# Values' projections as one 512-column product over both weight halves, and another order of work for the soft-max heads, in a two-layer hybrid encoder

## The chip, the cores and the metric

The kernel runs on one core of one Trainium2 chip. The metric is the device time of one execution in microseconds; less is better. The core has a matrix engine (TensorE, PE in the profile, with its weight loads shown apart as PEld), VectorE (DVE), ScalarE (ACT), GpSimd (POOL) and a queue that issues DMAs (SP). PE multiplies a moving operand by a stationary one of 128 x 128 and adds into PSUM; ACT and DVE read PSUM, POOL does not.

## The reference

Two layers work on x of 512 tokens by 1024. Each layer makes one wide projection of x, runs two groups of eight heads on it (head size 64), gates them, projects back and normalises:

```
proj = x @ w_in          # qA kA vA gA | qB kB vB gB | qI kI wI
A[t,s] = sigmoid(z[t,s]) * prod_{s<j<t} (1 - sigmoid(z[t,j])),  s < t      # group A, "sticks"
oA = A @ vA
score[t,s] = sum_h wI[t,h] relu(qI[t,h] . kI[s])                           # group B, soft-max heads
keep the 128 best admissible s of each t;  p = softmax(q.k/8 + bias[bucket(s-t)])
oB = p @ vB
x = LayerNorm(alpha * x + concat(oA*silu(gA), oB*silu(gB)) @ w_out)
```

All in float32.

## The kernel before

**Precision by halves.** A float32 operand is split into a high half (rounded to the type that PE multiplies at full rate, `fp32r`) and a low half (the rest). A product is three: high x high, low x high, high x low. So x lies in SBUF as `XH` and `XL`, and every weight chunk is split as it arrives: `raw` from DRAM, `whi` by ACT (L212), `wlo` by POOL (L215). Class `Stream` (L173) does this ahead of use, with two raw buffers and four buffers each for `whi` and `wlo`; its loads go out on SP in order.

**Units.** A projection unit is 256 columns of `w_in` for half of a group: (A or B, which four heads, q, k, v or g). q, k and gate units (`project_t`, L276) hold the weights still and move 512 tokens of x. Value units (`project_v`, L286) hold 128 tokens of x still and move 256 weight columns, so that values come out with tokens on partitions: four token blocks `tb`, each of eight chunks `kc` of the contraction, each chunk three matmuls (L303 to L305) into one PSUM tile `pjv`. The first unit of a layer, (A, 0, v), is joined with the indexer's keys (328 columns, weights in `joined`); the other three value units, (A, 1, v), (B, 0, v) and (B, 1, v), stand alone. The block's result is taken from PSUM ("eviction") by closures in the list `later`, which `flush()` calls at fixed places: for A, one ACT copy to `V_NOW` (L310), and after the last block a shift of the values by one row through three DMAs (`shift_values`) with differences two slots later; for B, `evac_v`: an ACT copy to the high half (L358), a DVE subtraction to the low half (L359). PSUM tiles for projections rotate through three buffers (`ppj`).

**Slots.** The order on PE, ACT, DVE and POOL is that of the program text; nothing is reordered. A layer runs 88 tasks, one a slot `s` (loop at L887): 24 for the indexer, then 64 for sixteen heads by four query blocks `qb`; heads 0 to 7 are sticks, 8 to 15 soft-max. A task's work is spread over slots: its scores z (`stage0`, PE) in its own slot; for a stick, sigmoid on ACT and one slot later a running product on DVE, transposes on PE three slots later (L526), their eviction to the buffers `AT` by ACT and DVE (L715, L718); for a soft-max task, bias and row minimum on DVE (L750), exponential on ACT (L755) in its own slot, transposes two slots later (L534, L537 evict them). After a head's fourth block comes `values()`, eight matmuls of AT by the values into `o` (L693), and `mix()`, which adds o's two halves and multiplies them into `M` (L595 on ACT, L597 on DVE, L598 on POOL). For sticks `values()` comes one slot after the last transposes and right behind the slot's own transposes; for soft-max heads one slot after the last transposes too, but at the slot's end, behind the fill.

**Fill.** Between these steps `fill(t)` issues projection matmuls, chunk by chunk, until their count of work (324 for a value chunk, 648 for others) reaches a target that is interpolated between pins (`HEAD_PINS`, `A_PINS`, `B_PINS`); so each unit has its slots: (A, 1, v) 35 to 38, (B, 0, v) 55 to 61, (B, 1, v) 70 to 77, and from slot 78 the first part of the output projection (`p1`). `fill` is called at 0.15, 0.55 and 1 of the slot; the call at 0.15 is left out where a stick is to be transposed.

**Top-k and biases.** From slot 24 to 51 `topk_rounds` puts the indexer's selection on DVE (L842, L843), about 1.5 rounds a slot; it ends in `mask[qb]`. A soft-max head's bias for a block is a strip of a table in DRAM (`f_dram`), read with one address step per row (tile `gbias`, L662) and used reversed. For heads 8 to 12 and two blocks of 15, POOL adds the mask (L741) or PE does; for heads 13, 14 and the other two blocks of 15, `STORED` names a place in `XN` (free then) where DVE adds table and mask ahead (L959) in slots 59 to 66, from tiles loaded at slots 57, 60 and 64 (`AHEAD`).

**Tail.** From slot 77 on, `mix_split` splits finished rows of M into XH and XL (L166, L167) for the output projection, the residual comes back into XN, and weights of `w_out` are split.

## Time and profile before

| what | value |
|---|---|
| median of 3 runs | 635.69 us (635.49 to 635.9) |
| the profiled execution | 635.7 us, span 633.9 us, granted clock 0.997 |
| PE busy | 624.9 us, 99% of the span |
| PEld, DVE, ACT, POOL busy | 547.0, 486.9, 343.2, 364.1 us |
| DMA | 77.41 MB, mean 122 GB/s |
| value matmuls of 256 columns (L303, L304, L305) | 192 each |

The span runs from the first to the last instruction of the profiled execution; the 1.8 us beside it are launch and end. A row of instructions names line, engine, operation, output and inputs with their shapes, how many there are, their busy time and the mean of one in ns, then the engine's idle time ahead of them and what ended it. In a timeline row the first figure is the start, the second the duration, and the bracket the idle time before it with its releaser. Matmuls overlap in the pipeline, so their spacing is read from starts. `z` are scores, `tr` transposes, `o` a head's output, `pj` and `pjv` projections, `pjo` the output projection.

### The profile page before, as it was taken

The numbers are of one execution on the slowest core, as the hardware profiler recorded it, in microseconds if no ns is written. First come the engines' busy times: TensorE is split into PE (matmuls) and PEld (weight loads), VectorE is DVE, ScalarE is ACT, GpSimd is POOL, SyncE is SP. The second block draws the span as 40 slices with busy tenths as digits, with TensorE's granted clock in tenths as the row PEclk, the third lists the DMA queues.
The fourth block names the chain that finished last, engine by engine and source line by source line (L and its number), as shares of the span: only waits on it lengthen the run. The fifth ranks groups of instructions, "written<-read, shape, count | busy, mean of one in ns | idle before, by whom it ended". The sixth has DMA issues, their size and how long they took to land.

```text
span 633.9 us, 10261 instructions
## 1 busy us (share of the span) xinstructions
PE 624.9 (99%) x3501; PEld 547.0 (86%) x3501; DVE 486.9 (77%) x1058; ACT 343.2 (54%) x686; POOL 364.1 (57%) x380
## 2 busy tenths in 40 slices
PE   9999999999999999999999999999999999999995
PEld 7988888988889889888899888899888898898884
DVE  3778999999966775668845789999998576656677
ACT  5686545544447466883135855554535566668700
POOL 5463544467466676798134544525674587778721
PEclk9999999999999999999999999999999999999998
DMA  7624343222263475353314342333133624634502
GB/s 237 214 79 133 100 133 101 82 86 68 99 169 94 120 188 168 119 192 119 133 67 132 103 132 99 100 100 106 62 101 116 167 85 137 173 126 144 168 34 99
DMA packets 31779, 77.41 MB, mean 122 GB/s; under 512 B 6572, under 2 KB 10668, under 8 KB 31728
## 3 DMA queue, kind: packets, MB, share of 16 engines
q1 hardware_dynamic: 31440, 76.51, 39.0%
q8 instruction: 27, 0.44, 0.3%
q10 hardware_dynamic: 288, 0.26, 0.1%
q14 instruction: 24, 0.20, 0.1%
HBM read 61.84 MB, written 4.44 MB: 105 GB/s over the span
## 4 chain that ended last, share of the span: by engine, by line
PE 92%; POOL 2%; ACT 2%; DMA 1%; DVE 1%; issue 1%; SPq 0%; DVEq 0%; POOLq 0%; ACTq 0%
PE pj L266 15%; PE pj L267 15%; PE pj L268 15%; PE pjo L797 12%; PE o L693 5%; PE tr L526 5%; PE z L521 4%; PE pjv L303 4%; PE z L518 4%; PE pjv L304 4%; PE pjv L305 4%; PE pjv L428 2%; POOL wlo L215 1%; PE pjq L430 1%; ACT p L755 1%
## 5 line engine op out<-in xcount | busy, mean ns | idle before, releaser
L215 POOL TENSOR_TENSOR wlo<-raw,whi 128x256 fp32r<-128x256 f32 (+1 forms) x250 | 225.0, 930 | 152.6 <-ACT whi L212 151.9
L266 PE MATMUL pj<-XH,whi 128*128 128x512 f32 (+1 forms) x432 | 171.5, 397 | 0.0
L267 PE MATMUL pj<-XL,whi 128*128 128x512 f32 (+1 forms) x432 | 166.4, 385 | 0.0
L268 PE MATMUL pj<-XH,wlo 128*128 128x512 f32 (+1 forms) x432 | 166.2, 385 | 0.0
L268 PEld LDWEIGHTS pj<-XH,wlo 128*128 128x128 f32 x432 | 81.1, 188 | 16.1
L267 PEld LDWEIGHTS pj<-XL,whi 128*128 128x128 f32 x432 | 81.4, 188 | 12.2
L266 PEld LDWEIGHTS pj<-XH,whi 128*128 128x128 f32 x432 | 81.3, 188 | 12.3
L705 ACT ACTIVATE om<-z 128x128 f32<-128x128 f32 (+1 forms) x64 | 28.0, 437 | 113.7 <-PE z L521 60.8
L212 ACT ACTIVATE whi<-raw 128x1024 fp32r<-128x1024 f32 x78 | 82.0, 1056 | 8.0 <-DMA raw<-in_w_in_dram 7.4
L598 POOL TENSOR_TENSOR M<-M,mixt 64x512 f32<-64x512 f32 x24 | 40.5, 1689 | 52.7 <-DVE mixt L597 41.3
L710 DVE TENSOR_TENSOR_SCAN om<-om,future 128x128 f32<-128x128 f32 (+1 forms) x64 | 63.6, 994 | 0.1
L303 PE MATMUL pjv<-whi,XH 128*128 128x256 f32 x192 | 56.9, 296 | 0.0
L305 PE MATMUL pjv<-wlo,XH 128*128 128x256 f32 x192 | 54.2, 283 | 0.0
L304 PE MATMUL pjv<-whi,XL 128*128 128x256 f32 x192 | 54.2, 282 | 0.0
L842 DVE MAX8 m<-scores 128x8 f32<-128x256 f32 (+2 forms) x96 | 52.8, 550 | 0.2
L843 DVE MATCH_REPLACE8 scores<-m,scores 128x256 f32<-128x256 f32 (+2 forms) x96 | 52.1, 543 | 0.0
L755 ACT ACTIVATE p<-p,mn 128x128 f32<-128x128 f32 (+1 forms) x64 | 35.8, 559 | 20.2 <-DVE mn L750 19.9
L693 PE MATMUL o<-AT,vt 128*128 128x512 f32 (+4 forms) x256 | 46.2, 322 | 0.0
L521 PE MATMUL z<-k,q 128*128 128x128 f32 (+3 forms) x128 | 41.7, 326 | 0.0
L797 PE MATMUL pjo<-whi,XH 128*128 128x512 f32 (+1 forms) x118 | 41.1, 387 | 0.0
L797 PE MATMUL pjo<-wlo,XH 128*128 128x512 f32 (+1 forms) x118 | 41.1, 384 | 0.0
L537 DVE TENSOR_TENSOR AT<-tr,AT 128x128 fp32r<-128x128 f32 (+1 forms) x64 | 31.2, 488 | 11.5 <-ACT AT L534 11.2
(165 smaller groups left out, 1286.7 us busy)
## 6 DMA issues: line engine op xcount, KB each, us to landing
raw<-in_w_in_dram SPq DMA_DIRECT2D x66, 512.0 KB, 3.3
k<-k SPq DMA_DIRECT2D x32, 256.0 KB, 5.5
raw<-in_w_out_dram SPq DMA_DIRECT2D x14, 512.0 KB, 3.2
gbias<-f_dram SPq DMA_DIRECT2D x18, 256.0 KB, 3.2
XN<-in_x_dram SPq DMA_DIRECT2D x8, 256.0 KB
y_dram<-XN SPq DMA_DIRECT2D x4, 512.0 KB, 2.6
XN<-y_dram SPq DMA_DIRECT2D x8, 256.0 KB, 3.7
M<-M SPq DMA_DIRECT2D x4, 448.0 KB
```

The lines of the kernel that those rows point to most:

```text
L212: A.activation(hi, src, AF.Copy)
L215: low = lambda lo=lo[:, c], src=src[:, c], hi=hi[:, c]: lo_engine.tensor_tensor(lo, src, hi, ALU.subtract)
L266: T.matmul(o, w[0], XH[:, tb:, kc, :], start=first, stop=False)
L267: T.matmul(o, w[0], XL[:, tb:, kc, :], start=False, stop=False)
L268: T.matmul(o, w[1], XH[:, tb:, kc, :], start=False, stop=last)
L303: T.matmul(full, XH[:, tb, kc, :], whi, start=kc == 0, stop=False)
L304: T.matmul(full, XL[:, tb, kc, :], whi, start=False, stop=False)
L305: T.matmul(full, XH[:, tb, kc, :], wlo, start=False, stop=kc == KC - 1)
L521: T.matmul(self.z[:, :nn], c, d, start=False, stop=True)
L693: T.matmul(self.o[:m, sb * P :], vt[:, sb, self.hh * P : self.hh * P + m], at_block(self.at[j], sb, sb, NTB - sb), start=n == 0, stop=n == 7)
L710: V.tensor_tensor_scan(rev, rev, future[:, S - n :][:, ::-1], 1.0, ALU.mult, ALU.max)
L797: T.matmul(acc[:, cols], mixed[:, tb, m, :], w[:, cols], start=n == 0, stop=n == len(steps) - 1)
```

## The change

1. **Value units that stand alone.** Their two weight halves are kept side by side: tile `w` of 2048 (formerly `whi` and `wlo` of 1024) is viewed as chunk, half, column, and `Stream.split` writes its two outputs there. A chunk's matmuls become two: XH by both halves, 512 columns, into the whole PSUM tile; XL by the high half, 256 columns, into its first half. In the last chunk the order is turned, so that the wide one ends the group. The two halves of the PSUM tile are added at eviction: `add_rest` copies the second half by ACT and adds it by DVE, for A straight into `V_NOW`, for B back into PSUM, with `evac_v` behind it. The joined first unit and all other units multiply as before.
2. **Slots.** For slots below 86, no fill at 0.15 where any task is to be transposed, and `values()` right behind the transposes for soft-max heads too; these come two slots after the last transposes now instead of one, and `mix()` with them. The last slots keep the old order.
3. **Stored biases.** The strips are loaded straight to their places in XN at slots 42, 44 and 46 (ten DMAs a layer), and DVE adds the masks in place, two sums a slot from slot 52. The three whole-width loads of `AHEAD` go away; the strips are read reversed where they are used.

```diff
--- before.py
+++ after.py
@@ -61,11 +61,12 @@
 
 
 STORED = {
-    13: {3: (59, 3, 0), 2: (59, 2, 0), 1: (60, 1, 0), 0: (60, 2, 384)},
-    14: {3: (62, 0, 512), 2: (62, 1, 512), 1: (63, 2, 512), 0: (63, 1, 896)},
-    15: {3: (66, 3, 512), 1: (66, 2, 768)},
+    13: {3: (3, 0), 2: (2, 0), 1: (1, 0), 0: (2, 384)},
+    14: {3: (0, 512), 2: (1, 512), 1: (2, 512), 0: (1, 896)},
+    15: {3: (3, 512), 1: (2, 768)},
 }
-AHEAD = {13: 57, 14: 60, 15: 64}
+STORE_SLOTS = {42: 13, 44: 14, 46: 15}
+SUM_AT = 52
 RESIDUAL = {(0, 0): 70, (0, 1): 78, (0, 2): 79, (0, 3): 80, (1, 1): 83, (1, 0): 84, (1, 2): 86, (1, 3): 88}
 SUM_SLOTS = 3
 HALF_SLOTS = 5
@@ -170,8 +171,15 @@
         nc.sync.dma_start(dst.bitcast(F32), src.bitcast(F32))
 
 
+    def weight_pair(name):
+        return wp.tile([P, 2048], F32R, tag="w", name=f"w{name}")
+
+    def halves(w):
+        return w[:, :1024], w[:, 1024:]
+
     class Stream:
-        def __init__(self, specs):
+        def __init__(self, specs, side_by_side):
+            self.side_by_side = side_by_side
             self.specs, self.raw, self.done, self.home = specs, {}, {}, {}
             self.loaded = self.ready = self.want = 0
             self.shared = set()
@@ -203,9 +211,13 @@
             if i in self.home:
                 pieces = self.home[i]
             else:
-                pieces = [[wp.tile([P, 1024], F32R, tag=tag, name=f"{tag}{i}") for tag in ("whi", "wlo")]]
-                self.done[i] = tuple(pieces[0])
-                pieces = [[t[:, :n].rearrange("p (a b) -> p a b", b=raw.shape[2]) for t in pieces[0]]]
+                w = weight_pair(i)
+                if i in self.side_by_side:
+                    self.done[i] = w = w.rearrange("p (a j b) -> p a j b", j=2, b=raw.shape[2])
+                    pieces = [[w[:, :, j, :] for j in range(2)]]
+                else:
+                    self.done[i] = halves(w)
+                    pieces = [[t[:, :n].rearrange("p (a b) -> p a b", b=raw.shape[2]) for t in self.done[i]]]
             k = raw.shape[1] // len(pieces)
             for j, (hi, lo) in enumerate(pieces):
                 src = raw[:, j * k : (j + 1) * k]
@@ -236,17 +248,19 @@
 
     units = [("A", 0, "v"), "ki", ("I", 0, "q")] + [u for u, _ in fills()]
 
-    specs, index = [], {}
+    specs, index, side_by_side = [], {}, set()
     for l in range(depth):
         for unit in units:
             index[l, unit] = len(specs)
             if unit == "ki":
                 specs.append((w_ki[l], 8 * 72))
             else:
+                if unit[2] == "v" and unit != units[0]:
+                    side_by_side |= {len(specs), len(specs) + 1}
                 specs += [(w_in[l, UNITS.index(unit), c], 1024) for c in range(2)]
         index[l, "o"] = len(specs)
         specs += [(w_out[l, half, mt], 1024) for half in range(2) for mt in range(4)]
-    stream = Stream(specs)
+    stream = Stream(specs, side_by_side)
 
 
     later = []
@@ -287,34 +301,46 @@
         i = index[l, unit]
         if keys is None:
             stream.prep(i + 1)
-            w = [[t.rearrange("p (a b) -> p a b", b=W256) for t in stream.done[i + h]] for h in range(2)]
+            w = [stream.done[i + h] for h in range(2)]
         else:
             stream.prep(i + 2)
             w = joined
-        n = w[0][0].shape[2]
         vv = vt.rearrange("p t (h r) -> p t h r", r=P)
         for tb in range(NTB):
             if tb:
                 stream.want = i + min(tb + 1, 3) + (keys is not None)
-            full = ppj.tile([P, S], F32, tag="pj", name="pjv")[:, :n]
-            acc = full[:, :W256]
+            full = ppj.tile([P, S], F32, tag="pj", name="pjv")
+            n = w[0][0].shape[2] if keys is not None else S
+            acc, rest = full[:, :W256], full[:, W256:]
             for kc in range(KC):
-                whi, wlo = (t[:, kc % 4, :] for t in w[kc // 4])
-                T.matmul(full, XH[:, tb, kc, :], whi, start=kc == 0, stop=False)
-                T.matmul(full, XL[:, tb, kc, :], whi, start=False, stop=False)
-                T.matmul(full, XH[:, tb, kc, :], wlo, start=False, stop=kc == KC - 1)
+                x = [t[:, tb, kc, :] for t in (XH, XL)]
+                if keys is not None:
+                    whi, wlo = (t[:, kc % 4, :] for t in w[kc // 4])
+                    products = ((full[:, :n], x[0], whi), (full[:, :n], x[1], whi), (full[:, :n], x[0], wlo))
+                else:
+                    both = w[kc // 4][:, kc % 4]
+                    products = ((full.rearrange("p (a b) -> p a b", b=W256), x[0], both), (acc, x[1], both[:, 0]))
+                    if kc == KC - 1:
+                        products = products[::-1]
+                for m, (o, a, b) in enumerate(products):
+                    T.matmul(o, a, b, start=kc == m == 0, stop=(kc, m) == (KC - 1, len(products) - 1))
                 if kc == KC - 1:
                     if keys is not None:
                         later.append(lambda tb=tb, full=full: keep_keys(tb, full))
-                    if unit[0] == "A":
                         later.append(lambda tb=tb, acc=acc: A.activation(V_NOW[:, tb, :], acc, AF.Copy))
+                    elif unit[0] == "A":
+                        later.append(lambda tb=tb, acc=acc, rest=rest: add_rest(V_NOW[:, tb, :], V_NOW[:, tb, :], acc, rest))
                     else:
+                        later.append(lambda tb=tb, acc=acc, rest=rest: add_rest(acc, tp.tile([P, S], F32, tag="t", name="rest")[:, :W256], acc, rest))
                         later.append(lambda tb=tb, acc=acc: evac_v(vv, tb, acc))
                 if (tb, kc) == (NTB - 1, KC - 1) and unit[0] == "A":
                     later.append(shift_values)
                     pending.append([SHIFT_SLOTS[1], lambda: value_steps(vv)])
-                yield 324 * n // W256
-
+                yield 324 * n // W256 if keys is not None else 324
+
+    def add_rest(out, place, acc, rest):
+        A.activation(place, rest, AF.Copy)
+        V.tensor_tensor(out, place, acc, ALU.add)
 
     V_NOW, V_PREV = (M[:, i : i + 2, :].rearrange("p x (y d) -> p (x y) d", d=W256) for i in (6, 4))
     pending = []
@@ -389,7 +415,7 @@
         unit = [index[0, u] for u in units[:3]]
         q_raw = vp.tile([P, NTB, 4 * P], F32, tag="v", name="q_raw").rearrange("p (c a) b -> p c (a b)", c=2)
         vk_raw = M.rearrange("p a b -> p (a b)")[:, : KC * (W256 + 72)].rearrange("p (a b) -> p a b", b=W256 + 72)
-        q_w = [tuple(wp.tile([P, 1024], F32R, tag=tag, name=f"{tag}q{c}") for tag in ("whi", "wlo")) for c in range(2)]
+        q_w = [halves(weight_pair(f"q{c}")) for c in range(2)]
         bias["oh"] = kp.tile([P, 4, S], F32, tag="k", name="oh").rearrange("p a b -> p (a b)")
         accs = [ppj.tile([P, S], F32, tag="pj", name="pjv") for _ in range(3)]
         q_accs = [pz.tile([P, S], F32, tag="z", name="pjq") for _ in range(2)]
@@ -656,10 +682,13 @@
                 return q, self.s, k, 2 * self.s
 
             def load(self):
+                self.g = gp.tile([P, S], F32, tag="g", name="gbias")
+                self.fetch(self.g)
+
+            def fetch(self, place):
                 h = 4 * self.i + self.hh
-                self.g = gp.tile([P, S], F32, tag="g", name="gbias")
                 base = f_dram[h : h + 1, 0:S]
-                nc.sync.dma_start(self.g, bass.AP(tensor=base.tensor, offset=base.offset, ap=[[1, P], [1, S]]))
+                nc.sync.dma_start(place, bass.AP(tensor=base.tensor, offset=base.offset, ap=[[1, P], [1, place.shape[1]]]))
 
             def begin(self):
                 self.late = (self.pair, self.s) != (7, 1)
@@ -733,8 +762,8 @@
                 self.p = wk.tile([P, S], F32, tag="w", name="p")
                 self.apart = bool(stored) and self.qb not in stored
                 if self.qb in stored:
-                    _, tb, col = stored[self.qb]
-                    self.bias = XN[:, tb, col : col + self.n]
+                    tb, col = stored[self.qb]
+                    self.bias = XN[:, tb, col : col + self.n][:, ::-1]
                     return
                 self.bias = h.g[:, : self.n][:, ::-1]
                 if not self.apart:
@@ -833,6 +862,7 @@
                 else:
                     st["done"] += step
 
+        sums = []
         rounds = [qb for _ in range(TOPK // 8) for qb in range(1, NTB)]
 
         def topk_rounds(upto):
@@ -896,9 +926,10 @@
                     stream.prep_ahead()
             now = s + (s >= IDX_SLOTS)
             sticks = [at(s - i) if isinstance(at(s - i), Stick) else None for i in (3, 4)]
-            softs = [at(s - i) if isinstance(at(s - i), Soft) else None for i in (2, 3)]
+            softs = [at(s - i) if isinstance(at(s - i), Soft) else None for i in (2, 4 if s < SLOTS - 2 else 3)]
             olds = [t for t in (sticks[0], softs[0]) if t]
             ended = [t if t and t.qb == NTB - 1 else None for t in (sticks[1], softs[1])]
+            joined_run = bool(olds) and s < SLOTS - 2
             done = ended[0] or ended[1]
             if at(s):
                 tasks[s].stage0()
@@ -911,12 +942,12 @@
             if isinstance(at(s + 1), Soft):
                 tasks[s + 1].prepare()
             flush()
-            if not sticks[0]:
+            if not joined_run:
                 fill(now + FRAC[0])
             for old in olds:
                 old.transpose()
                 old.evacuate(old.head.at)
-            if ended[0]:
+            if done and s < SLOTS - 2:
                 done.head.values()
             if behind:
                 tasks[s - 1].stage2()
@@ -935,7 +966,7 @@
                 stream.home[o0 + 10] = [[t[:, :, W256:] for t in joined[i]] for i in range(2)]
                 lows = []
                 stream.split(o0 + 8, lows=lows)
-            if ended[1]:
+            if done and s >= SLOTS - 2:
                 done.head.values()
             if done:
                 mix(done.head.pair, done.head.s, done.head.o, V if last else G)
@@ -950,13 +981,15 @@
             for place, by in RESIDUAL.items():
                 if s == by:
                     load_residual(l, *place)
-            for h in STORED:
-                if s == AHEAD[h]:
-                    by_number[h].load()
-                for qb, (by, tb, col) in STORED[h].items():
-                    if s == by:
-                        n = P * (qb + 1)
-                        V.tensor_tensor(XN[:, tb, col : col + n], by_number[h].g[:, :n][:, ::-1], mask[qb], ALU.add)
+            if s in STORE_SLOTS:
+                h = STORE_SLOTS[s]
+                for qb, (tb, col) in STORED[h].items():
+                    by_number[h].fetch(XN[:, tb, col : col + P * (qb + 1)])
+                    sums.append((XN[:, tb, col : col + P * (qb + 1)], mask[qb][:, ::-1]))
+            if s >= SUM_AT:
+                for place, hidden in sums[:2]:
+                    V.tensor_tensor(place, place, hidden, ALU.add)
+                del sums[:2]
             if l == 0 and s in (10, 14):
                 make_future(s == 14)
             if l == 0 and s in (3, 6):
```

## The prediction

> **What bounds the kernel now.** I read the page first (engine totals, granted clock, chain), then the waits of the weight loads, then single rows of the timeline.
>
> ```profile
> span 633.9 us, 10261 instructions
> PE 624.9 (99%) x3501; PEld 547.0 (86%) x3501; DVE 486.9 (77%) x1058; ACT 343.2 (54%) x686; POOL 364.1 (57%) x380
> ...
> PEclk9999999999999999999999999999999999999998
> ...
> PE 92%; POOL 2%; ACT 2%; DMA 1%; DVE 1%; issue 1%; SPq 0%; DVEq 0%; POOLq 0%; ACTq 0%
> ```
>
> TensorE is busy 99% of the span at full clock and is 92% of the chain. Its weight loads wait for other engines at a handful of places only:
>
> ```profile
> PEld tr L526 <- ACT p L765: 1.2, 3, 0.5
> ...
> PEld o L693 <- DVE AT L537: 0.3, 2, 0.2
> PEld tr L526 <- ACT p L755: 0.3, 2, 0.2
> ```
>
> So time is won by shortening TensorE's own stream, and lost wherever another engine falls behind it. Busy rows overstate a matmul (they are pipelined); what counts is start to start:
>
> ```profile
> 200.74 0.28 PE L303 MATMUL pjv<-whi,XH 128*128 128x256 f32 x1
> 200.85 0.28 PE L304 MATMUL pjv<-whi,XL 128*128 128x256 f32 x1
> 200.97 0.28 PE L305 MATMUL pjv<-wlo,XH 128*128 128x256 f32 x1
> ...
> 202.17 0.28 PE L303 MATMUL pjv<-whi,XH 128*128 128x256 f32 x1
> ```
>
> ```profile
> 151.69 0.39 PE L266 MATMUL pj<-XH,whi 128*128 128x512 f32 x1
> ...
> 153.74 0.39 PE L266 MATMUL pj<-XH,whi 128*128 128x512 f32 x1
> ```
>
> ```profile
> 71.23 0.39 PE L268 MATMUL pj<-XH,wlo 128*128 128x512 f32 x1
> 71.46 0.28 PE L518 MATMUL z<-k,q 128*128 128x256 f32 x1
> 71.57 0.28 PE L521 MATMUL z<-k,q 128*128 128x256 f32 x1
> 71.69 0.40 PE L266 MATMUL pj<-XH,whi 128*128 128x512 f32 x1
> ```
>
> From 200.74 to 202.17 lie 12 matmuls of 256 columns: 1.43 / 12 = 119 ns each, 357.5 ns a chunk of three. From 151.69 to 153.74 lie 9 of 512: 228 ns each. The third fence is the only place where 256 columns follow 512: 110 and 120 ns.
>
> **The change part by part.**
>
> *Matmuls.* 6 units (three value projections in each of two layers) x 4 token blocks x 8 chunks = 192 chunks; the rows of the eviction groups below count their blocks, 8 (of the 12 at L310) and 16. A chunk goes from 3 x 256 columns to 512 + 256: the same columns, one weight load and one matmul fewer. New form, so bounds: 228 plus 110 to 120 is 338 to 348; I take 228 + 117 = 345, since half the 256-column matmuls will have a 512 on both sides as at 71.57. Saved: 357.5 - 345 = 12.5 ns (9.5 to 19.5), 32 x 12.5 = 0.40 us a unit, 2.4 us in all (1.8 to 3.7). Turning the last chunk round moves one 256 beside another and costs nothing I can see. The planner still counts 324 a chunk, so units keep their slots.
>
> The Trainium skill ("TensorE: Matmul & The Clock Gate", Back-to-back issue gap) gives a warm gap of N/2.4 + 2.5 ns. By it, as an estimate, a chunk goes from 327 to 325 ns and the whole change saves 0.5 us; our rows, 119 and 228 ns, lie above its 109 and 216, more so at 256 columns, so here a matmul fewer is worth more than the page says.
>
> *Eviction.*
>
> ```profile
> L359 DVE TENSOR_TENSOR vt<-pjv,vt 128x256 fp32r<-128x256 f32 x16 | 6.7, 420 | 1.1 <-ACT vt L358 1.1
> ...
> L358 ACT ACTIVATE vt<-pjv 128x256 fp32r<-128x256 f32 x16 | 6.0, 373 | 1.4 <-PE pjv L305 1.4
> ...
> L310 ACT ACTIVATE M<-pjv 128x256 f32<-128x256 f32 x12 | 4.6, 381 | 16.5 <-DVE heads L551 14.2 <-PE trx L1051 2.3
> ```
>
> Each of the 8 sticks' blocks gains one DVE add (as L359, 0.42 us); each of the 16 soft-max blocks gains an ACT copy (0.38) and a DVE add, and its copy to high halves now stands in ACT's queue until DVE has added, about 0.8 us later than today. The PSUM buffer is held that much longer; there are three and a block takes some 3 us, so nothing waits for it. The question is where 1.7 us of DVE (4 adds) or 3.2 us of ACT lateness a unit finds slack. Three places.
>
> (1) Sticks' unit (slots 35 to 38), in the top-k stretch:
>
> ```profile
> 108.50:131.20 22.70, 22.70 (x164) 21.30 (x163) 21.87 (x48) 10.75 (x23) 10.44 (x12) 1.00 0.23 75
> ```
>
> ```profile
> 132.31 0.69 DVE L582 TENSOR_TENSOR sig<-pj,sig 128x512 f32<-128x512 f32 x1 [1.17 <-ACT sig L580]
> ...
> 137.93 0.66 DVE L718 SCALAR_TENSOR_TENSOR AT<-tr,AT 128x512 fp32r<-128x512 f32 x1
> ```
>
> ```profile
> 138.29 1.47 PE L693 MATMUL o<-AT,vt 128*128 128x512 f32 x8
> ```
>
> DVE (third figure of the window, 21.87 of 22.70) is full. The four adds, some 0.34 each in the stream (rows there overlap by 0.08), are 1.35 us; the one pause behind them is the 1.17 before L582. So L718 ends about 0.2 later than 138.59. The product at 138.29 reads that result in its third matmul, behind one of 512 and one of 384 columns and the turn from the transposes, at 138.78 in the trace: slack 0.19 less a semaphore's way, say 0.13. Queued behind the adds on DVE are the scans that the transposes wait for, but those are read three slots on. TensorE, 0.40 early, then waits 0.2 + 0.4 - 0.13 = 0.47. **The unit's gain is eaten here**, once a layer; bounds: nothing eaten, to 0.5 beyond the gain if one of DVE's rows stretches, as 256 and 384 columns at L959 below do (1651 ns for 384, 686 for 512). The shift of the values by one row, three DMAs, starts behind the last add, 1.3 us later than now; its reader is held back two slots by the kernel, so that costs nothing.
>
> (2) First soft-max unit (slots 55 to 61), where the bias sums go away and others come before:
>
> ```profile
> L959 DVE TENSOR_TENSOR XN<-gbias,mask 128x384 f32<-128x384 f32 x4 | 6.6, 1651 | 0.0
> ...
> L959 DVE TENSOR_TENSOR XN<-gbias,mask 128x256 f32<-128x256 f32 x6 | 5.1, 856 | 0.0
> ...
> L959 DVE TENSOR_TENSOR XN<-gbias,mask 128x512 f32<-128x512 f32 x6 | 4.1, 686 | 0.1
> ```
>
> ```profile
> 200.12 0.56 DVE L750 CUSTOM_DVE_ANT_0 p<-z,p 128x384 f32<-128x384 f32 x1 [1.36 <-PE z L521]
> ...
> 201.09 0.69 DVE L718 SCALAR_TENSOR_TENSOR AT<-tr,AT 128x512 fp32r<-128x512 f32 x1
> ```
>
> ```profile
> 203.13 0.65 PE L693 MATMUL o<-AT,vt 128*128 128x512 f32 x2
> ```
>
> The ten sums, 15.8 / 2 = 7.9 us a layer and a little for 128 columns, move from slots 59 to 66 to slots 52 to 56, two a slot. The last four (some 2.4 us) and the first add arrive before 201.09, against a pause of 1.36: L718 ends some 1.5 late, at 203.3, for a read at 203.6 that comes up to 0.4 earlier. It just fits (0 to 0.3 lost); I take 0. Keeps 0.40 a layer.
>
> The sums' data now comes by ten loads at slots 42 to 46 in place of three whole-width loads (heads 13 to 15, at 57 to 64). Each issue holds SP 0.33:
>
> ```profile
> L662 SPq DMA_DIRECT2D gbias<-f_dram x18: 321/326/1576, 175.1 to 543.7; - x18
> ```
>
> Four in a row are 1.3 us ahead of a weight load that is fetched two chunks (over 10 us) early: no cost while that cover holds, 1.3 us once a slot if not.
>
> (3) Second soft-max unit (slots 70 to 77) and what follows, where ACT decides:
>
> ```profile
> 572.49 0.59 ACT L595 ACTIVATE mixt<-o 64x512 f32<-64x512 f32 x1
> 572.99 1.05 ACT L212 ACTIVATE whi<-raw 128x1024 fp32r<-128x1024 f32 x1
> 574.06 0.38 ACT L534 ACTIVATE AT<-tr 128x256 fp32r<-128x256 f32 x1
> 574.52 0.73 ACT L755 ACTIVATE p<-p,mn 128x512 f32<-128x512 f32 x1
> ```
>
> ```profile
> 573.12 0.68 DVE L597 TENSOR_TENSOR mixt<-o,mixt 64x512 f32<-64x512 f32 x1 [0.93 <-ACT mixt L595]
> 573.74 0.68 DVE L750 CUSTOM_DVE_ANT_0 p<-z,XN 128x512 f32<-128x512 f32 x1
> ```
>
> ```profile
> 575.39 0.20 PEld L526 LDWEIGHTS tr<-ident,p 128*128 128x128 f32 x2 [0.16 <-ACT p L755]
> ...
> 591.74 0.42 PEld L526 LDWEIGHTS tr<-ident,p 128*128 128x128 f32 x4 [0.52 <-ACT p L765]
> ```
>
> The exponentials end at 574.52 + 0.73 = 575.25 and TensorE waits for them: no slack. Here the slot's order helps. The head's output product and its mix move one slot on, so L595 (0.59) leaves the queue ahead of 574.52, and L750 no longer stands behind L597 with its 0.93 pause. Against that, the last block's copy and add push the queue by some 0.3 net (part of 0.8 falls into ACT's present pauses). 0.59 - 0.3: the exponentials come 0.3 to 0.4 earlier, as TensorE does. Keeps 0.40 a layer, and since L212 and the low halves behind it also move up, the stall at 591.74 (0.25 over the usual transpose gap) shrinks: 0.2 a layer.
>
> *Slot order otherwise.* Transposes come straight after the score product instead of behind a part of the fill (the last slots keep the old order): the number of turns between transposes, products and projections stays, so TensorE's cost is 0; the exponentials are needed a little sooner, which matters only where (3) has no slack, and there no fill stood between even before. Side-by-side halves: same bytes, same instructions, 0.
>
> **Sum**, on the profiled execution's 635.7 (span 633.9, 1.8 around it; the median of the runs is 635.69): sticks' units 0, soft-max units 4 x 0.40 = 1.6, end stalls 2 x 0.2 = 0.4. 635.7 - 2.0 = **633.7**.
>
> **Rivals.**
>
> *Everything kept*: DVE makes up its adds before 138.29. For: the next heads' slack is 2 us. Against: the window above. 2.4 + 0.4: 632.9, by the best bound of the spacing 631.6.
>
> *Only the first soft-max unit pays*: the second unit's ACT work just cancels the moved mix, 575.25 stays. 635.7 - 0.8 = 634.9.
>
> *512 columns over two halves cost what two 256 cost*, 2 x 119: then a chunk is 357 again, and with the end stalls it is 635.3. For: nothing but that the form is new; against: 228 at 512 with the same operand type. The Trainium skill's formula would end near there too, by another way.
>
> *Slower*: ACT's in-order wait for DVE's add. Place: slots 72 to 78; price 0.8 a block, 3.2 a layer, if none falls into pauses; less the 0.59 + 0.93 given back by the mix it is 1.7 late at 575.39, twice 3.4, less the first unit's 0.8: 638.3. It decides as soon as the lateness exceeds what the mix gives back, and ACT's pauses in
>
> ```profile
> 557.00:575.40 18.40, 18.40 (x140) 17.38 (x139) 10.78 (x37) 14.37 (x36) 13.90 (x13) 1.00 0.43 140
> ```
>
> (18.40 - 14.37 = 4.0 us) speak against its full price.
>
> **How the numbers follow.** Forecast 0.40, everything kept 0.25, only one unit 0.20, 512 dear 0.08, slower 0.07. Range: 632.0 takes in most of the all-kept case, 635.6 the two small ones. 0.2% (1.3 us) is about what a measurement of this kernel tells from no change, so faster means below 634.4: forecast and all-kept, 0.65; same: the next two, 0.28; slower 0.07.
>
> **What would show it.** Right: matmul count 3501 - 192 = 3309; chunks of 345 ns; a TensorE wait of about half a microsecond for DVE's L718 at the sticks' fourth head's output product, in each layer; the wait of 0.52 for L765 gone or smaller. Wrong: no wait there (then 632.9), 256-column matmuls of 119 and 512 above 228 (then the spacing), new waits for ACT's exponentials between slots 72 and 81, or weight loads waiting for SP after slot 42.

## The result: slower by 1.3%, and the profile after

The changed kernel takes 644.19 us (median of four runs, 644.05 to 644.45) against 635.8 us in the runs of before beside it: ratio 1.0133, 95% interval 1.0121 to 1.0145. Forecast were 633.7 us, and the range ended at 635.6. The page of the changed kernel begins:

```profile
span 642.4 us, 9944 instructions
...
PE 627.5 (98%) x3309; PEld 536.5 (84%) x3309; DVE 491.0 (76%) x1082; ACT 346.5 (54%) x702; POOL 367.2 (57%) x380
```

192 matmuls fewer, as forecast, and the timeline of value chunks has them at the spacing that was taken (start, duration, engine and line):

```profile
250.63 0.40 PE L326 MATMUL pjv<-w,XH 128*128 128x512 f32 x1
...
250.98 0.39 PE L326 MATMUL pjv<-w,XH 128*128 128x512 f32 x1
...
251.32 0.40 PE L326 MATMUL pjv<-w,XH 128*128 128x512 f32 x1
```

Two chunks in 0.69 us are 345 ns each. A whole unit gains less than 32 times the 12.5 ns: where no wait stands, in the sticks' unit, it is 0.29 us in each layer and not 0.40 (from slot 35 to slot 40, by the starts of each slot's first score product, here and before). The loss is in the waits of TensorE's weight loads (us in total, times, longest):

```profile
PEld tr L552 <- ACT p L784: 4.6, 6, 1.5
PEld tr L552 <- ACT p L794: 2.9, 6, 0.6
PEld tr L552 <- DVE AT L747: 2.8, 4, 1.1
...
PEld z L544 <- DVE mn L779: 1.1, 4, 0.4
PEld o L722 <- DVE vt L385: 0.9, 2, 0.5
```

Together 12.3 us; the answering waits of before, 1.2 + 0.3 + 0.3, were 1.8. So 10.5 us of waits are new; the span grew by 8.5, since the value units gained a part back. Taken from the starts of the slots' first score products, against before, the 8.5 us stand here:

| stretch | layer 0 | layer 1 |
|---|---|---|
| slots 58 and 59 | +1.10 | +1.10 |
| slots 76 to 79 | +2.81 | +2.77 |
| from slot 84 to the next layer, or to the last matmul | +0.58 | +0.71 |
| all other slots, the value units' gain among them | -0.71 | -0.70 |

The rest is 0.2 us ahead of slot 24, where the traced executions lie up to 0.45 us from before in either direction, and 0.6 us behind the last matmul.

**Slots 74 to 79.** Timeline rows of the changed kernel, ordered by engine; the bracket is the idle time before and what ended it:

```profile
249.76 2.54 POOL L227 TENSOR_TENSOR w<-raw,w 128x512 fp32r<-128x512 f32 x2 [1.08 <-ACT w L224]
252.27 2.05 POOL L770 TENSOR_TENSOR p<-gbias,mask 128x384 f32<-128x384 f32 x2
...
253.22 0.56 DVE L779 CUSTOM_DVE_ANT_0 p<-z,p 128x384 f32<-128x384 f32 x1 [2.33 <-POOL p L770]
253.70 0.42 DVE L343 TENSOR_TENSOR pjv<-rest,pjv 128x256 f32<-128x256 f32 x1
...
257.88 0.69 DVE L623 TENSOR_TENSOR mixt<-o,mixt 64x512 f32<-64x512 f32 x1 [0.90 <-ACT mixt L621]
259.28 0.42 DVE L343 TENSOR_TENSOR pjv<-rest,pjv 128x256 f32<-128x256 f32 x1
260.54 0.56 DVE L563 TENSOR_TENSOR AT<-tr,AT 128x384 fp32r<-128x384 f32 x1
...
250.54 0.38 ACT L342 ACTIVATE rest<-pjv 128x256 f32<-128x256 f32 x1
254.16 0.38 ACT L384 ACTIVATE vt<-pjv 128x256 fp32r<-128x256 f32 x1 [3.24 <-DVE pjv L343]
...
257.88 0.39 ACT L342 ACTIVATE rest<-pjv 128x256 f32<-128x256 f32 x1
259.74 0.38 ACT L384 ACTIVATE vt<-pjv 128x256 fp32r<-128x256 f32 x1 [1.48 <-DVE pjv L343]
...
261.24 0.30 PE L552 MATMUL tr<-ident,p 128*128 128x128 f32 x1 [1.20 <-DVE AT L563]
```

ACT has copied the second half of the block (L342) and its next instruction, the copy to the high half (L384), needs DVE's sum of the halves (L343). That sum stands in DVE's order behind a row minimum, which waits for POOL's bias sum, which stands behind POOL's weight split: ACT is idle for 3.24 us. One block later the sum stands behind the head's mix, and ACT is idle for 1.48 us. What stands behind L384 on ACT and DVE, the eviction of transposes (L563 at 260.54) and exponentials, is late; the transposes at 261.24 have no free PSUM buffer until L563 is done. The exponential that they read is late as well: it ends on ACT at 260.79, L563 at 261.10. The weight load's row names the one (L784), the matmul's row the other. That one wait costs 1.4 us a layer.

**Slots 56 to 59**, the same view:

```profile
197.96 1.52 DVE L991 TENSOR_TENSOR XN<-XN,mask 128x512 f32<-128x512 f32 x2
199.41 0.41 DVE L779 CUSTOM_DVE_ANT_0 p<-z,p 128x256 f32<-128x256 f32 x1
...
201.77 0.43 DVE L343 TENSOR_TENSOR pjv<-rest,pjv 128x256 f32<-128x256 f32 x1 [1.00 <-ACT rest L342]
202.65 0.43 DVE L385 TENSOR_TENSOR vt<-pjv,vt 128x256 fp32r<-128x256 f32 x1 [0.45 <-ACT vt L384]
203.14 0.69 DVE L747 SCALAR_TENSOR_TENSOR AT<-tr,AT 128x512 fp32r<-128x512 f32 x1
...
199.92 0.51 ACT L784 ACTIVATE p<-p,mn 128x256 f32<-128x256 f32 x1 [1.51 <-DVE mn L779]
200.43 1.04 ACT L224 ACTIVATE w<-raw 128x1024 fp32r<-128x1024 f32 x1
201.38 0.36 ACT L342 ACTIVATE rest<-pjv 128x256 f32<-128x256 f32 x1
...
203.88 0.44 PE L552 MATMUL tr<-ident,p 128*128 128x128 f32 x2 [0.61 <-DVE AT L747]
```

Two bias sums (1.5 us) hold DVE's row minimum back, ACT idles 1.51 us for it and only then splits weights for 1.04 us; the block's eviction behind that takes two turns between ACT and DVE, and the sticks' last transposes leave PSUM 0.6 to 0.8 us too late.

### The profile page after: what moved, and what is told of

The parts are those of the page before. It is cut to its first block, busy times and chain, and to the rows that moved or that the text cites. A ratio compares the mean times of both kernels' runs of the same rounds, so it can differ in the third digit from the quotient of the medians.

```text
span 642.4 us, 9944 instructions
## 1 busy us (share of the span) xinstructions
PE 627.5 (98%) x3309; PEld 536.5 (84%) x3309; DVE 491.0 (76%) x1082; ACT 346.5 (54%) x702; POOL 367.2 (57%) x380
## 5 line engine op out<-in xcount | busy, mean ns | idle before, releaser
L227 POOL TENSOR_TENSOR w<-raw,w 128x256 fp32r<-128x256 f32 (+1 forms) x250 | 229.9, 949 | 157.4 <-ACT w L224 150.2
L280 PE MATMUL pj<-XH,w 128*128 128x512 f32 (+1 forms) x432 | 171.1, 396 | 0.0
L281 PE MATMUL pj<-XL,w 128*128 128x512 f32 (+1 forms) x432 | 166.5, 385 | 0.0
L282 PE MATMUL pj<-XH,w 128*128 128x512 f32 (+1 forms) x432 | 166.3, 385 | 0.0
L282 PEld LDWEIGHTS pj<-XH,w 128*128 128x128 f32 x432 | 81.2, 188 | 16.1
L281 PEld LDWEIGHTS pj<-XL,w 128*128 128x128 f32 x432 | 81.4, 188 | 12.9
L280 PEld LDWEIGHTS pj<-XH,w 128*128 128x128 f32 x432 | 81.4, 188 | 12.6
L224 ACT ACTIVATE w<-raw 128x1024 fp32r<-128x1024 f32 x78 | 82.0, 1056 | 10.0 <-DMA raw<-in_w_in_dram 9.7
L326 PE MATMUL pjv<-w,XH 128*128 128x512 f32 x192 | 71.3, 407 | 0.0
L826 PE MATMUL pjo<-w,XH 128*128 128x512 f32 (+1 forms) x236 | 68.9, 384 | 0.0
L326 PE MATMUL pjv<-w,XL 128*128 128x256 f32 x192 | 50.3, 281 | 0.0
L826 PEld LDWEIGHTS pjo<-w,XH 128*128 128x128 f32 x236 | 43.2, 189 | 7.4
L784 ACT ACTIVATE p<-p,mn 128x128 f32<-128x128 f32 (+1 forms) x64 | 35.9, 561 | 20.1 <-DVE mn L779 19.4
L563 DVE TENSOR_TENSOR AT<-tr,AT 128x128 fp32r<-128x128 f32 (+1 forms) x64 | 31.3, 489 | 14.0 <-ACT AT L560 13.3
```

The costliest lines, as they stand in the source:

```text
L224: A.activation(hi, src, AF.Copy)
L227: low = lambda lo=lo[:, c], src=src[:, c], hi=hi[:, c]: lo_engine.tensor_tensor(lo, src, hi, ALU.subtract)
L280: T.matmul(o, w[0], XH[:, tb:, kc, :], start=first, stop=False)
L281: T.matmul(o, w[0], XL[:, tb:, kc, :], start=False, stop=False)
L282: T.matmul(o, w[1], XH[:, tb:, kc, :], start=False, stop=last)
L326: T.matmul(o, a, b, start=kc == m == 0, stop=(kc, m) == (KC - 1, len(products) - 1))
```

## Experiments

Medians in us; the ratio is to runs of before on the same chip.

| kernel | median | ratio, 95% interval |
|---|---|---|
| products alone | 642.82 | 1.0111 [1.0096, 1.0126] |
| order alone | 642.4 | 1.0104 [1.0089, 1.0119] |
| stored biases alone | 636.82 | 1.0014 [1.0005, 1.0024] |
| products and order | 654.09 | 1.0294 [1.0274, 1.0313] |
| order and biases | 636.72 | 1.0015 [1.0006, 1.0025] |
| products, two-turn eviction | 638.0 | 1.0038 [1.0023, 1.0053] |
| the same and biases | 640.42 | 1.0075 [1.006, 1.009] |
| whole change, two-turn eviction | 642.15 | 1.0103 [1.0086, 1.012] |
| products, last block as before | 640.04 | 1.0062 [1.0049, 1.0074] |
| the same, two-turn eviction | 635.91 | 0.9998 [0.9989, 1.0007] |
| whole change, last block as before | 643.27 | 1.0111 [1.0097, 1.0125] |
| whole change, sums a slot earlier | 642.36 | 1.0103 [1.0089, 1.0117] |
| sticks' unit alone | 635.23 | 0.9991 [0.9982, 1.0001] |
| sticks' and first soft-max unit, two-turn, last block as before | 635.84 | 1.0 [0.9991, 1.0009] |

**Products alone.** The eviction and `Stream` of the change; `STORED`, `AHEAD` and the slot loop of before:

```diff
+                    products = ((full.rearrange("p (a b) -> p a b", b=W256), x[0], both), (acc, x[1], both[:, 0]))
...
+                        later.append(lambda tb=tb, acc=acc, rest=rest: add_rest(acc, tp.tile([P, S], F32, tag="t", name="rest")[:, :W256], acc, rest))
                         later.append(lambda tb=tb, acc=acc: evac_v(vv, tb, acc))
```

> The 512-column products with their longer eviction alone; slots and stored biases as before. Theory A (the eviction's second turn: ACT waits in its queue for DVE's add, and DVE's late low halves hold the transposes' buffers): most of the loss is here, 639 to 643 us. Theory B (the new slot order makes transposes and values come too early): TensorE keeps its saving, 633 to 635 us. Theory C (the bias sums moved to slots 52 to 56 make DVE late at the first soft-max unit): 633 to 635 us as well.

642.82 us, in the range of theory A. The timeline of this kernel at slot 62:

```profile
213.69 0.38 ACT L341 ACTIVATE rest<-pjv 128x256 f32<-128x256 f32 x1
214.56 0.38 ACT L383 ACTIVATE vt<-pjv 128x256 fp32r<-128x256 f32 x1 [0.49 <-DVE pjv L342]
...
214.98 0.42 DVE L384 TENSOR_TENSOR vt<-pjv,vt 128x256 fp32r<-128x256 f32 x1 [0.45 <-ACT vt L383]
...
215.46 0.67 PE L718 MATMUL o<-AT,vt 128*128 128x128 f32 x3 [1.38 <-DVE vt L384]
```

From 213.69, where the copy to the high half would have stood, the four turns take until 215.40; the output product reads the unit's last block and waits. By starts (a matmul's start less the one that the usual spacing gives) this costs 1.54 us in slot 62 and 1.06 in slot 78, and the transposes of 77 wait 0.5. So the products lose 7 us without any help from the order.

**Order alone.** The loop's edits of the change (`softs`, `joined_run`, `values()`), the rest as before:

```diff
-            softs = [at(s - i) if isinstance(at(s - i), Soft) else None for i in (2, 3)]
+            softs = [at(s - i) if isinstance(at(s - i), Soft) else None for i in (2, 4 if s < SLOTS - 2 else 3)]
...
-            if not sticks[0]:
+            if not joined_run:
```

> The new slot order alone, with the old three products and old biases. Theory A: 635 to 636 us, no difference or a little faster. Theory B: 638 to 642 us, with waits of transposes at slots 78 and 79. Theory C: 635 to 636 us.

642.4 us, near theory B's range, but not by waits at slots 78 and 79: those aren't there. Nearly all of it is one place of each layer: TensorE waits in slot 66, 2.7 us by starts, for what stands behind DVE's bias sums of slot 63 (the first row is the group of DVE's old bias sums: shortest, median and longest in ns; then the timeline):

```profile
L960 DVE TENSOR_TENSOR XN<-gbias,mask x20: 277/723/5383, 206.6 to 546.9; 128x512 f32<-128x512 f32 x6, 128x256 f32<-128x256 f32 x6, 128x384 f32<-128x384 f32 x4, 128x128 f32<-128x128 f32 x4
```

```profile
220.21 5.71 DVE L960 TENSOR_TENSOR XN<-gbias,mask 128x256 f32<-128x256 f32 x2
...
220.36 1.41 POOL L598 TENSOR_TENSOR M<-M,mixt 64x512 f32<-64x512 f32 x1 [2.67 <-DVE mixt L597]
221.74 2.52 POOL L215 TENSOR_TENSOR wlo<-raw,whi 128x512 fp32r<-128x512 f32 x2
224.22 2.72 POOL L741 TENSOR_TENSOR p<-gbias,mask 128x256 f32<-128x256 f32 x3
...
226.52 0.44 PE L518 MATMUL z<-k,q 128*128 128x384 f32 x1 [0.86 <-DVE mn L750]
```

The second of the two sums, 128 columns, takes 5.38 us where the shortest of its group takes 0.28. It runs while POOL works without a pause from 220.36 to 226.94. The new order puts POOL's mix at that place; before, the mix had run at 216.78, and POOL stood idle for 2.25 us when the same two sums ran at 219.76 in 0.61 us.

**Stored biases alone.** The loads and sums of the change, products and order of before:

```diff
-            for h in STORED:
-                if s == AHEAD[h]:
...
+            if s >= SUM_AT:
+                for place, hidden in sums[:2]:
+                    V.tensor_tensor(place, place, hidden, ALU.add)
```

> The new loads and sums of the stored biases alone. Theory A and B: 635.5 to 636 us. Theory C: 637 to 638 us, with TensorE waiting in slots 58 and 59 of both layers for some 1 us each.

636.82 us, by the ratio 0.9 over before and between the ranges of the theories. Two places of the trace make it up: slot 58 is 0.2 us longer in each layer, and 0.6 us lie behind the last matmul. From that matmul's start to the end of the span, each kernel traced with the new biases takes 8.2 us and each without them 7.6, whatever else was changed; why isn't shown.

**Products and order**, the whole change without its biases:

```diff
+AHEAD = {13: 57, 14: 60, 15: 64}
-STORE_SLOTS = {42: 13, 44: 14, 46: 15}
-SUM_AT = 52
```

> Products and slot order, biases as before, so the changed kernel less its bias sums. Theory C: 641.5 to 642.5 us, 2 us below the changed kernel, because the waits in slots 58 and 59 go. Theories A and B: 644 us as the changed kernel.

654.09 us, 9.9 more than the whole change and not what any of the theories had: moving the sums is what saves the order from slot 66. The collision of the order alone is here too (the two sums take 5.67 us). TensorE waits twice, and its matmuls slow down (rows of this kernel's timeline):

```profile
227.53 0.69 PE L543 MATMUL z<-k,q 128*128 128x384 f32 x1 [2.52 <-DVE mn L775]
...
229.53 0.45 PE L551 MATMUL tr<-ident,p 128*128 128x128 f32 x1 [0.99 <-DVE AT L562]
...
230.63 0.63 PE L281 MATMUL pj<-XH,w 128*128 128x512 f32 x1
231.06 0.63 PE L279 MATMUL pj<-XH,w 128*128 128x512 f32 x1
```

0.43 us apart instead of 0.23, for some ten matmuls, in both layers; the granted clock there is 0.50.

**Order and biases**, the whole change with the matmuls, weights and eviction of before:

```diff
-                        later.append(lambda tb=tb, acc=acc, rest=rest: add_rest(acc, tp.tile([P, S], F32, tag="t", name="rest")[:, :W256], acc, rest))
                         later.append(lambda tb=tb, acc=acc: evac_v(vv, tb, acc))
```

> The new slot order and the stored biases' new loads and sums, without the 512-column products. The order alone took 642.4 us for one collision (VectorE's bias sum of slot 66 took 5.4 us beside GpSimd's work); the biases alone 636.8 us. If that collision is all that the order costs, moving the sums to slots 52 to 56 takes it away: 636 to 637.5 us, no wait over 0.3 us, and the products add the other 7 us of the change. Rival 'the order costs by itself': 639 us or more, with the waits at slots 78 and 79.

636.72 us, as expected: with the sums out of the way the order costs nothing (the biases alone took 636.82), and the products add 7.5 us to these two. At the layer's end it is 0.5 and 0.3 us longer than before (from slot 84 on, layers 0 and 1), where the products alone lose nothing: what the change loses there does not come from the products alone. Its rows where the changed kernel's ACT idled 1.48 us:

```profile
254.60 0.59 ACT L596 ACTIVATE mixt<-o 64x512 f32<-64x512 f32 x1
255.22 0.39 ACT L359 ACTIVATE vt<-pjv 128x256 fp32r<-128x256 f32 x1
255.50 0.49 ACT L535 ACTIVATE AT<-tr 128x384 fp32r<-128x384 f32 x1
```

The mix, the copy to the high half and the eviction of transposes follow each other without a pause.

**Two turns instead of four.** ACT copies the high half and the rest one behind the other; DVE subtracts and adds alone:

```diff
-                        later.append(lambda tb=tb, acc=acc, rest=rest: add_rest(acc, tp.tile([P, S], F32, tag="t", name="rest")[:, :W256], acc, rest))
-                        later.append(lambda tb=tb, acc=acc: evac_v(vv, tb, acc))
+                        later.append(lambda tb=tb, acc=acc, rest=rest: evac_halves(vv, tb, acc, rest))
+        A.activation(hi, heads(acc), AF.Copy)
+        A.activation(t, rest, AF.Copy)
+        V.tensor_tensor(heads(t), heads(t), hi, ALU.subtract)
+        V.tensor_tensor(lo, heads(acc), heads(t), ALU.add)
```

With the products alone:

> The 512-column products with the two-turn eviction, slot order and stored biases as before. The products alone took 642.8 us, with output products waiting 1.54 us (slot 62) and 1.06 us (slot 78) for the low or high half's eviction. Theory 'second turn': both waits shrink under 0.3 us and the products' gain of some 2.4 us shows: 634 to 636.5 us. Rival 'values follow too closely on the last block, whoever evicts it': they stay over 1 us, 640 to 643 us.

638.0 us: 4.8 us of the products' 7.0 are back, more than the rival allows, less than expected. The wait of slot 62 falls from 1.54 to 0.47, that of slot 78 stays (1.1). Slot 62 in its timeline:

```profile
213.22 1.08 DVE L391 TENSOR_TENSOR rest<-rest,vt 128x256 f32<-128x256 f32 x1 [0.22 <-ACT rest L390]
214.34 0.42 DVE L392 TENSOR_TENSOR vt<-pjv,rest 128x256 fp32r<-128x256 f32 x1
...
212.73 2.72 POOL L226 TENSOR_TENSOR w<-raw,w 128x512 fp32r<-128x512 f32 x2 [2.50 <-ACT w L223]
```

The subtraction has both inputs in SBUF and takes 1.08 us beside POOL's weight split, the addition with one input in PSUM 0.42.

With the biases as well:

> The 512-column products with the two-turn eviction and the stored biases of the changed kernel, but the slot order of before. Theory 'second turn': as the products alone with that eviction, and 0.5 to 1.5 us on top from the 512-wide sums and their place (the biases alone cost 1.0 us): 635 to 638 us. Rival 'the order is what makes the changed products bearable': the output products' waits of slots 62 and 78 stay over 1 us and it is over 641 us.

640.42 us, between the two. The wait of slot 59 is back at 1.13 us, that of slot 78 is 1.12, that of slot 62 gone.

In the whole change:

> The whole change, but the soft-max units' eviction in two turns instead of four: ScalarE copies the high half from PSUM and the rest to SBUF one behind the other, then VectorE subtracts and adds; ScalarE never waits for VectorE. Theory 'second turn' (ScalarE stands in its order for VectorE's add, and what is behind it comes late): the waits of slots 58, 59 and 78 (1.06 and 1.37 us in each layer of the changed kernel) go, 4 to 5 us in all: 637 to 640 us. Rival 'VectorE's added work' (the 512-wide sums and the wider task are late because VectorE has more to do): it has one operation more here, so the waits stay or grow: 643 to 647 us.

642.15 us, 2.0 less than the change and also between the two. The transposes' wait of slot 78 falls from 1.37 to 0.5, the one of slot 59 grows from 0.78 to 1.12. So the second turn is part of the loss in the whole change, not all of it. DVE has one operation more in this form; what that costs by itself wasn't isolated.

**The last block as before.** In the soft-max units the fourth block goes by three matmuls of 256 and `evac_v`:

```diff
+        return unit[0] == "B" and tb == NTB - 1
...
+                    elif short(unit, tb):
+                        later.append(lambda tb=tb, acc=acc: evac_v(vv, tb, acc))
```

With the products and their four turns for the other blocks:

> The same with the changed kernel's own four-turn eviction for the blocks before the last. Theory 'the last block': the output products' waits of slots 62 and 78 (1.54 and 1.06 us) go; the transposes' waits of slots 77 and 78 (0.5 and 0.2 us), which earlier blocks cause, stay: 634.5 to 635.7 us. Theory 'second turn': the turn costs wherever it stands, so over 637 us.

With two turns for the other blocks:

> The 512-column products with the two-turn eviction, slot order and stored biases as before, but the last token block of each soft-max unit goes as before: three 256-column products and one copy and one subtraction to evict it. Theory 'the last block' (what costs is that the output products stand ready right behind the last block, so its longer eviction shows in full): the waits of slots 62 and 78 go, and the gain of three units less two blocks' 0.1 us each shows, 0.8 to 1.0 us a layer: 633.9 to 634.5 us. Rival 'any wider block delays the queue of ScalarE there' (the wait of slot 78 ended on a transposes' copy, not on the value): it stays over 0.7 us in each layer, 635.5 us or more.

640.04 and 635.91 us. The weight loads' waits for low halves at output products, with the products alone, then in these two kernels:

```profile
PEld o L718 <- DVE vt L384: 5.4, 4, 1.6
```

```profile
PEld o L723 <- DVE vt L389: 1.8, 4, 0.7
```

```profile
PEld tr L564 <- ACT p L793: 0.7, 2, 0.4
...
PEld o L731 <- DVE vt L388: 0.4, 2, 0.2
```

The four-turn kernel keeps a wait of 0.64 in slot 62, so earlier blocks' turns reach the last one: here the theory of the second turn holds, at 4.1 us between these two kernels. With two turns the time is that of before, 1.4 us over the expectation and in the rival's range, though without the wait of 0.7 at slot 78 that the rival asked for. By the starts of its score products this kernel has gained 0.6 us in each layer up to slot 78; slot 78 takes 0.26 of it back, slot 81, with a transposes' wait of 0.34, another 0.2.

The same edit in the whole change:

> The whole change, but the last token block of each soft-max unit by three 256-column products with the old eviction. Theory 'the last block': of the 8.4 us lost against before, the waits of slots 78 and 79 (about 2.3 us a layer) go, those of slots 58 and 59 (1.06 us a layer, by the stored biases' sums) stay: 639 to 641 us. Rival 'the new order is at fault at slot 78' (transposes one slot later hold the buffer whatever the values' eviction does): 643 us or more.

643.27 us. The wait of 1.37 at slot 78 is untouched: blocks before the last cause it, as the rows of 253 to 260 us above have it. The rival was right on the place; that the order alone is at fault is refuted by order and biases, which have no such wait. It takes both.

**Sums one slot earlier**, in the whole change:

```diff
-SUM_AT = 52
+SUM_AT = 51
```

> The whole change with the stored biases' sums one slot earlier (from slot 51 instead of 52, so that the last pair, 512 and 256 wide, is in slot 55's order instead of 56's). Theory 'late start plus longer queue' (in the changed kernel these two sums, 1.19 and 0.41 us, keep ScalarE idle 1.5 us before the exponential of slot 57; the first values' eviction then starts some 2.5 us later than in the kernel with the products alone, and only with the two added turns it reaches the transposes of slot 59): the waits of slots 58 and 59 (0.28 and 0.78 us a layer) go, slots 78 and 79 stay as they are: 641.5 to 642.6 us. Rival 'the values' eviction alone makes slot 59 late': they stay, 643.7 to 644.6 us.

642.36 us, as expected: the waits of slots 58 and 59 go but for 0.1 us, those of 78 and 79 are as they were.

**Sticks' unit alone.** Products and add for (A, 1, v), everything else as before:

```diff
+                if unit[2] == "v" and unit[0] == "A" and unit != units[0]:
```

> Only the sticks' values unit (slots 35 to 38) takes 512-column products; both soft-max units, the slot order and the stored biases as before. By the marks of the changed kernel that unit gained 0.29 us in each layer with no wait behind it: 635.1 to 635.4 us. Rival, the prediction's own step (the fourth head's output product waits for VectorE's low half and takes the gain back): 635.7 to 636.1 us, with a wait at that product near 138 us. Either way none of the waits of slots 58, 59, 62 and 78 is there.

635.23 us. Score products at slots 32 and 48 of layer 0, before and here:

```profile
96.78 0.22 PE L518 MATMUL z<-k,q 128*128 128x128 f32 x1
...
159.62 0.22 PE L518 MATMUL z<-k,q 128*128 128x128 f32 x1
```

```profile
97.06 0.22 PE L545 MATMUL z<-k,q 128*128 128x128 f32 x1
...
159.62 0.22 PE L545 MATMUL z<-k,q 128*128 128x128 f32 x1
```

The unit gains 0.28 us in this layer, as much in the other, and nothing takes it back. DVE's row at which the kernel before paused 1.17 us has no pause here:

```profile
132.30 0.69 DVE L609 TENSOR_TENSOR sig<-pj,sig 128x512 f32<-128x512 f32 x1
```

**Two units**: the sticks' unit, and the first soft-max unit with two turns and its last block as before:

```diff
+        return unit == ("B", 1, "v") or unit[0] == "B" and tb == NTB - 1
```

> Slot order and stored biases as before; 512-column products for the sticks' unit and for the first three token blocks of the first soft-max unit, with its two-turn eviction; the second soft-max unit and every last block as before. By the slot marks of the kernel with the last blocks short, the first soft-max unit gains 0.18 us a layer more than the sticks' unit alone, and what the second unit gains is lost at slots 78 and 81. If that holds and the waits of 78 and 81 belong to the second unit: 634.7 to 635.1 us, no wait over 0.3 us before slot 86. Rival, the waits of slots 78 and 81 come from the first unit's later state: 635.4 to 636 us.

635.84 us. The waits of slots 78 and 81 are gone, so they belonged to the second unit; the time is still that of before, as the rival has it, but without its waits. In its trace each layer has gained 0.45 us by slot 84 and keeps it until there; from slot 84 on 0.2 and 0.4 us go again (layers 0 and 1), and 0.37 us were lost ahead of slot 24, within what executions differ there. Why the layers end later isn't shown. No kernel tried is faster than the one before by more than the measurement tells; the sticks' unit alone comes nearest, and its interval just reaches 1.

## Why the prediction was wrong

*Matmuls: right in number and spacing, too large for a unit.* 3309 of them, 345 ns a chunk in a run of chunks; but the sticks' unit gained 0.28 us, not 0.40, some 9 ns a chunk.

*Step 1, sticks' unit, "The unit's gain is eaten here": wrong.* No wait stands at the fourth head's output product; the unit keeps its 0.28 us. The adds came in where they were put, but did not delay DVE by four times 0.34: the pause of 1.17 held them all.

*Step 2, first soft-max unit, "It just fits": wrong.* It costs 1.06 us a layer at slots 58 and 59. The step counted the sums and the add as DVE's work, 1.5 us, and left out the way over ACT: the exponential behind the sums, the weight split of 1.04 behind that, then the copy, and the wait of 0.45 for the second copy. L747 starts at 203.14 and ends at 203.83, not at the 203.3 of the step. The step looked at the output product that reads L747's result; first to wait are the transposes ahead of it, which need the PSUM buffer that L747 empties, from 203.1 on. Moving the sums by one slot removes both waits but for 0.1 us, and 1.8 us of the time.

*Step 3, second soft-max unit and what follows: the step that failed most.* It was to keep 0.40 us a layer and win 0.2 at the end; slots 76 to 79 lose 2.8 and the end 0.6 to 0.7. "Here the slot's order helps": the mix was to leave ACT's and DVE's queues earlier. Instead DVE's add stands behind the mix or behind a row minimum that waits for POOL, and ACT stands behind the add. The delay was put at 0.8 us less pauses, for the last block alone; ACT's two idle times are 3.24 and 1.48 us, and blocks before the last suffice for the wait of 1.37. What appeared is the step's own sign of being wrong, waits for late exponentials between slots 72 and 81. The stall at the end grew too (L794 2.9 us, against 1.2 of L765).

*Eviction: "nothing waits for it" was right of `pjv`'s buffers and asked for the wrong one.* The buffers that ran short are those of the transposes, which are evicted behind it in the same two queues.

*"Slot order otherwise: 0": right only together with the moved sums* (order and biases 636.72, biases alone 636.82). With the old sums it costs 6.6 us.

*The slower rival* (ACT's in-order wait, slots 72 to 78) named the mechanism and the place. It was priced at 638.3 and 0.07 because ACT's 4.0 us of pauses were read as room. ACT then idled for 3.24 us in one piece, in its own order behind L342; that pauses of this kind move along with DVE, and so are no room, is read from these rows and was not tested by itself. What decided was the time between turns on a loaded DVE, not the 0.8 us that four turns take by themselves: with two turns 4.8 us came back with the products alone, but only 2.0 in the whole change.

## What to carry to other kernels

An eviction that goes ACT, DVE, ACT, DVE ties both in-order queues to whatever stands ahead of each turn; cost each added turn at the longest wait ahead of it in the other queue, not at its own duration. A gain of some 9 ns a chunk is worth a longer eviction only where the result is needed late: here the sticks' unit, whose values are read some slots later, kept its 0.28 us in the trace; the soft-max units, whose values are multiplied right behind the last block, lost far more with four turns, and even with two turns and a short last block did not come out ahead. When steps are moved together, ask which of them only repairs another: the sums' move cost 0.9 us alone and saved 9.9 in company.

## What was not expected of the hardware

A DVE operation with both inputs in SBUF can be held over several POOL instructions that follow each other without a pause: 0.28 us became 5.38, in an interval in which POOL finished five instructions (the mix, two weight splits, two of three bias sums), and a 256-column subtraction 1.08 beside a weight split; an add of the same size with an input in PSUM took 0.42 beside the same split. The Trainium skill ("SBUF — State Buffer", Who interferes with whom and Summary) states the contention for two SBUF inputs against a POOL operation that reads SBUF, and the traces agree on which operation suffers; it lets the later one wait until the first is done, and here the wait went on over four more.

In the kernel with products and order, the granted clock of TensorE is 0.50 from 227.3 to 234.1 us and in a like stretch of layer 1, and some ten matmuls run at about half speed there (0.43 us for 512 columns); the mean over that execution was 0.988. The clock falls while TensorE is in the first wait, of 2.5 us: it is still 1.00 at 226.0 to 227.2, with that wait under way, and 0.50 before the score product of 227.53. The second wait, of 1.0 us, comes at half clock already. Waits of 1.4 us by the same kind of row (products alone in slot 62, order alone in slot 66) were followed by no such stretch. Where between 1.4 and 2.5 us the limit lies, and what else it depends on, isn't shown.
